# A reordered front, twenty zero products and a later overflow loop in a layer with a recurrence, cross-attention and 64 experts

## Chip, cores, metric

The kernel runs on one core of a Trainium2 chip. The metric is the device time of one execution in microseconds (us). A profile of one execution, taken by the hardware profiler, stands beside the times.

## What is computed

One layer for 256 tokens of width 1024, all in float32:

```python
u = rmsnorm(h, norm1_w)
rx, rg, qkv, z, a, b, ga, gb = split(u @ w_in)
rx = causal_dwconv(rx, w) + bias            # 4 taps
h_rnn = rglru(rx, ...)                      # linear recurrence along the tokens, 1280 channels
y_a = (gelu(rg) * h_rnn) @ w_branch_a
q, k, v = split(silu(causal_dwconv(qkv)))   # 8 heads of 128
o = gated_delta_rule(l2norm(q), l2norm(k), v, g(a), sigmoid(b))   # chunks of 64
y_b = (rmsnorm(o) * silu(z)) @ w_branch_b
h = h + (sigmoid(ga) * y_a + sigmoid(gb) * y_b) @ w_out
h = h + cross_attention(rmsnorm(h), rmsnorm(mem))   # 4 heads, 256 memory tokens
h = h + hier_moe(rmsnorm(h))  # best of 8 groups, then best 2 of its 8 experts; SwiGLU, 512 wide
return rmsnorm(h)
```

## The kernel before

The core has engines that run side by side, each with its own queue in a fixed order: TensorE (PE) multiplies, VectorE (DVE), ScalarE (ACT) and GpSimd (POOL) do the rest, and SyncE (SP) issues most loads. The program is written in a tile framework. A planner there fixes each engine's order ahead of time: it goes by the order in which the code names the operations, lets an operation inside `tc.high_priority()` go ahead, and puts a ready one in front of one that its own cost estimates hold to be late. Tiles come from pools with a few buffers, and a tile waits until the buffer's last user is done. A loop whose count is only known at run time (`tc.For_i`) is a block of its own, and nothing is planned across it.

*The front.* Its dense products come in units. A unit loads 1 MB of weights on SP (`load_w`, line 162), splits them into a high and a low half (`whl`: the high half on ACT, line 169; the low half for one part on DVE and for the other on POOL, line 170), and multiplies in 48 steps of 128 by 256 (`dense`, lines 178 to 180) into a bank of PSUM (`mm`, four of them). After that comes the unit's own work:

- 5 x units: the convolution (`conv`) on ACT and with six steps on DVE, into `xc`;
- 5 gelu units (`g_unit`): three steps on ACT and DVE in turn, into `gg`;
- `memory_norm` (the norm of the memory tokens, and keys `KT` scaled by it) and `smalls` (constants of the recurrence);
- `recurrence(h)`, twice, for five blocks of 128 channels each: 10 products into banks `gd` (line 385), tanh and exp on ACT (lines 386 to 393), eight long steps on DVE over 128 by 1280 (lines 394 to 404), a split into `ghh` and `ghl`;
- `decay` (the decay factors of the delta rule), and 4 value units (`value_unit`), which make the memory's values with one scaled copy on ACT;
- 12 k, q and v units (`qkv_unit`): convolution and SiLU on ACT and DVE at high priority, with `z_unit(0)` ahead of the second, `key_sums` behind the eighth (line 496) and `query_sums` behind the tenth (line 519);
- 8 short units for `wa`, which need both recurrences' results, then the delta rule with the remaining units, `wb`, `wo`, the attention, `wco`.

The order before is: x units with `memory_norm` behind the first, `smalls`, gelu units, both recurrences, `decay`, value units, and then the twelve units. Tiles of the front that live long come from a pool of ten buffers (`early`).

*The choice.* With the last `wco` unit the router's logits are done. Four PSUM banks `into` are opened with a product by zeros each (line 81). DVE then finds group and experts (lines 962 to 988, at high priority), TensorE counts the places of the tokens (lines 990 to 995), and `xe0`, the tokens of expert 0, is gathered (line 1045).

*The experts.* Each of 64 experts has three weight tiles of 2 MB (gate, up, down), 192 in all, which go through a ring of ten tiles: four in pool `ra`, six in pool `rb`, which lies where the front's weights were. `load_next` issues them on SP in order (lines 1101 to 1109); a load waits until its tile has been read by the expert ten tiles earlier. The expert `e` (`expert(e)`) multiplies its up to 32 tokens with gate and up (`gate_up`, line 1140, 64 products each), makes the hidden values, multiplies with down (line 1160) and keeps the rows in `Y`. After every fourth expert `combine` adds four experts' rows into `into` (line 1176), and `prepare` gathers the tokens of the next four into `xe`: two comparisons on DVE for every second call (line 1002), a scale (line 1123) and 32 products (line 1131).

*The overflow.* An expert with more than 32 tokens needs further blocks. Their number `nblk` is counted in the choice, and `overflow` runs a loop over it:

```python
n = nc.values_load(nblk[0:1, 0:1], ...)     # line 1235
with tc.For_i(0, n, 1):                     # line 1236
    ...                                     # picks the block's expert, loads its weights by SP, adds its rows
```

With these inputs the body isn't entered. It uses the memory of `xe` for its weights. Before, `overflow()` stands ahead of the experts.

Of the kernel before, what the change touches and what calls it, by code (L numbers as in the profile page):

```python
# [41 lines left out]
def hybrid_kernel(ctx: ExitStack, tc: tile.TileContext, A, out, dbg=None, until=99):  # L42
    nc = tc.nc
    V, SC, G, T = nc.vector, nc.scalar, nc.gpsimd, nc.tensor
# [291 lines left out]
    def smalls():  # L336

        V.tensor_scalar_mul(ch[:, 0], P("lam"), -1.0)
        softplus(ch[:, 1], ch[:, 0], ch[:, 2], ch[:, 3], ch[:, 4])
        V.tensor_scalar_mul(ch[:, 0], ch[:, 1], -4.0)  # L340
        V.tensor_scalar_mul(ch[:, 1], ch[:, 1], 2.0)
        V.tensor_scalar_mul(hb[:, 0], P("ba"), 0.5)
        V.tensor_scalar_mul(hb[:, 1], P("bx"), 0.5)
# [35 lines left out]
    def recurrence(h):  # L379
        tr, ti = five("tr"), five("ti")  # L380
        for b in range(HB):
            r = h * HB + b
            p = bank("gd")
            for s in range(2):
                T.matmul(p[:, s * 256:s * 256 + 256], wg[h][:, s, b], xc[h][:, b], start=True, stop=True)
                SC.activation((tr, ti)[s][:, b], p[:, s * 256:s * 256 + 256], AF.Tanh,
                              bias=hb[:, s, r:r + 1], scale=0.5)

        a = five("lra")
        for b in range(HB):  # L390
            r = h * HB + b
            SC.activation(a[:, b], tr[:, b], AF.Exp, bias=ch[:, 0, r:r + 1], scale=ch[:, 0, r:r + 1])
            SC.activation(tr[:, b], tr[:, b], AF.Tanh, bias=ch[:, 1, r:r + 1], scale=ch[:, 1, r:r + 1])
        V.scalar_tensor_tensor(tr, a, 1.0, tr, op0=OP.add, op1=OP.mult)
        V.tensor_scalar(a, tr, -1.0, 1.0, op0=OP.mult, op1=OP.add)
        V.scalar_tensor_tensor(tr, tr, -2.0, tr, op0=OP.add, op1=OP.mult)

        SC.activation(tr, tr, AF.Sqrt, scale=-1.0 / 16)
        V.scalar_tensor_tensor(ti, ti, 1.0, xc[h], op0=OP.add, op1=OP.mult)
        V.tensor_mul(ti, ti, tr)  # L400
        V.memset(a[:, :, 0:1], 0.0)
        flat = lambda t: t.rearrange("p b t -> p (b t)")
        V.tensor_tensor_scan(flat(tr), flat(a), flat(ti), 0.0, OP.mult, OP.add)
        V.tensor_mul(ti, tr, gg[h])
        dump(f"gh{h}", ti)
        hi, lo = five("ghh", FR), five("ghl", FR)
        split(hi, lo, ti)
        gh.append((hi, lo))
# [16 lines left out]

    for un_ in range(5):
        x_unit(un_)
        if un_ == 0:
            memory_norm()
    smalls()  # L430
    for un_ in range(5):
        g_unit(un_)
    for h in range(2):
        recurrence(h)
    decay()
    for un_ in range(4):
        value_unit(un_)
    if until <= 1:
        return

# [71 lines left out]
    def query_sums():  # L512
# [8 lines left out]
        V.tensor_scalar(NK[:, 1], pss[:, :16], 0.25, EPS, op0=OP.mult, op1=OP.add)  # L521
        V.tensor_scalar_mul(NK[:, 1], NK[:, 1], 2048.0 * EPS)

    for un_ in range(12):
        if un_ == 1:
            z_unit(0)
        qkv_unit(un_)
        if un_ == 7:
            key_sums()
        if un_ == 9:  # L530
            query_sums()
# [415 lines left out]

    into = [[opened(bank(), 512) for _ in range(2)] for _ in range(2)]


    LA = small("rla", [2, 72])
    LG, LE = LA[:, :, :8], LA[:, :, 8:].rearrange("p t (g j) -> p t g j", g=8)
# [235 lines left out]
    def prepare(k):  # L1188

        if k < NE // 4:  # L1190
            if k % 2 == 0:
                g, pw = picked if k == 0 else (onehot(k * 4, 8), None)
                pw = pw or weighted(k // 2, g)
                oh[k // 2] = g, pw.rearrange("p (t x) -> p t x", t=2)
            gather(xe, oh[k // 2][0][:, :, k % 2 * 128:k % 2 * 128 + 128], 128)

    def expert(e, last=None):
        g8, i = divmod(e, 8)
        x = xe[:, :, i % 4 * 32:i % 4 * 32 + 32] if e else xe0
        p = bank("gd")  # L1200
        for k in range(2):
            m = gate_up(p, k * 128, x, ring[3 * e + k], range(8))
        if e == 2:
            pin = tc.keep_in_program_order
            pin(m)
            for tt in range(2):
                for h in range(2):
                    pin(T.matmul(into[tt][h], ident, hm[:, tt].rearrange("p (c q) -> p q c", c=8)[:, h * 64:h * 64 + 64],  # L1208
                             start=False, stop=False, skip_group_check=True))
        ht = hidden(p)  # L1210
        if last:
            return last(ht, [last_columns(ring[3 * e + 2], q) for q in LAST])
        p = bank("gd")
        down(p, ht, ring[3 * e + 2], range(4))
        to_rows(Y, 32 * (i % 4), p)
        for _ in range(3):
            load_next()
        if i % 4 == 3 or e == NE - 2:
            n = 32 * (i % 4 + 1)
            combine(lambda tt: oh[g8][1][:, tt, 32 * (i + 1) - n:32 * (i + 1)], Y, n)  # L1220
        if e == 0:
            prepare(0)
        if i % 4 == 3:
            prepare(e // 4 + 1)

# [45 lines left out]
            to_rows(Y, 0, p)  # L1271
            combine(lambda tt: opw[:, tt], Y, SLOTS)

    overflow()
    for e in range(NE - 3):
        expert(e)

# [159 lines left out]
```

## Time and profile before

| | |
|---|---|
| time, median of 3 runs | 1500.93 us (1498.08 to 5531.12) |
| the profiled execution | 1499.66 us, span 1497.9 us |
| mean granted TensorE clock | 0.885 |
| busy: PE, DVE, ACT, POOL | 1109.8, 539.3, 349.4, 199.9 us |
| read from memory | 474.17 MB |

The span runs from the first to the last instruction of the profiled execution, and the time of that execution has a little around it. Busy shares are means over very different parts: in the front DVE and PE are busy, in the expert part the DMA engines.

### The profile page before, as it was taken

To read this page: it belongs to the slowest core of one execution; us is meant where nothing else is said; L and a number is where in the kernel's file an instruction comes from. 1 tells how busy PE (TensorE), PEld (TensorE's weight loads), DVE (VectorE), ACT (ScalarE), POOL (GpSimd) and SP (SyncE) were. 2 spreads that over 40 slices of the span, in tenths; PEclk is the share of its full clock that TensorE was granted. 3 is DMA by queue.
4 is the path that set the end of the run, shared out by engine and by line. 5 is a ranking of instruction groups with operands and counts; after the bars stand their busy time and mean duration, and the time that the engine had idled before them with its cause. 6 is when DMAs were issued, how large, how long until landed. Compare 5 with 4: busy or idle time off the path is not lost.

```text
span 1497.9 us, 33194 instructions
## 1 busy us (share of the span) xinstructions
PE 1109.8 (74%) x14941; PEld 929.0 (62%) x14941; DVE 539.3 (36%) x1217; ACT 349.4 (23%) x741; POOL 199.9 (13%) x107
## 2 busy tenths in 40 slices
PE   6998999979999957876565675756656756666575
PEld 6997999979889945654444553545544545445453
DVE  7966786675757332221111211111202111111122
ACT  5356664417435510100000000000000000000011
POOL 2443332621136200000000000000000000000000
PEclk9999998989999978998898887887979889789897
DMA  7343352521268367999999999999999999999994
GB/s 254 138 170 130 123 170 92 191 85 58 84 243 325 116 273 327 426 425 425 426 426 427 425 427 424 425 426 427 425 426 425 426 426 427 425 425 427 426 424 177
DMA packets 42002, 477.40 MB, mean 319 GB/s; under 512 B 4481, under 2 KB 7169, under 8 KB 9857
## 3 DMA queue, kind: packets, MB, share of 16 engines
q1 hardware_dynamic: 40560, 472.56, 76.9%
q8 instruction: 119, 1.95, 0.5%
q10 hardware_dynamic: 1296, 2.68, 0.5%
q14 instruction: 27, 0.21, 0.0%
HBM read 474.17 MB, written 1.05 MB: 317 GB/s over the span
## 4 chain that ended last, share of the span: by engine, by line
DMA 56%; PE 5%; DVE 0%; issue 0%; ACT 0%; DVEq 0%; SPq 0%; ACTq 0%
DMA rb<-wed 13%; DMA rb<-weu 11%; DMA rb<-weg 11%; DMA ra<-weu 8%; DMA ra<-weg 8%; DMA ra<-wed 5%; PE gd L1140 2%; PE gd L1160 1%; PE mm L1176 1%; PE gd L1131 1%; PE mm L1208 0%; ACT fsq L1329 0%; DVE goh L1002 0%; PE gd L1313 0%; PE mm L1322 0%
## 5 line engine op out<-in xcount | busy, mean ns | idle before, releaser
L1140 PE MATMUL gd<-rb,xy 128*32 128x128 f32 x4864 | 182.0, 314 | 112.7 <-DMA rb<-weu 56.8
L1140 PEld LDWEIGHTS gd<-rb,xy 128*32 128x32 f32 x4864 | 160.1, 127 | 140.1 <-DMA rb<-weu 65.0
L170 POOL TENSOR_TENSOR whl<-raw,whl 128x1024 fp32r<-128x1024 f32 (+1 forms) x66 | 161.5, 2448 | 328.5 <-ACT whl L169 324.9
L1149 DVE SCALAR_TENSOR_TENSOR hid<-hid,gd 128x128 f32<-128x128 f32 x64 | 18.4, 288 | 440.7 <-ACT hid L1148 440.7
L1140 PE MATMUL gd<-ra,xy 128*32 128x128 f32 x3168 | 120.3, 317 | 72.4 <-DMA ra<-weg 35.2
L180 PE MATMUL mm<-u1h,whl 128*128 128x256 f32 x544 | 159.0, 292 | 6.9 <-DVE whl L170 6.4
L1140 PEld LDWEIGHTS gd<-ra,xy 128*32 128x32 f32 x3168 | 106.3, 128 | 88.6 <-DMA ra<-weu 40.1
L179 PE MATMUL mm<-u1l,whl 128*128 128x256 f32 x544 | 159.9, 294 | 0.0
L178 PE MATMUL mm<-u1h,whl 128*128 128x256 f32 x544 | 159.4, 293 | 0.0
L169 ACT CAST whl<-raw 128x1024 fp32r<-128x1024 f32 (+1 forms) x132 | 131.1, 1007 | 118.5 <-PE mm L180 87.9
L1148 ACT ACTIVATE hid<-gd 128x128 f32<-128x128 f32 x64 | 17.7, 277 | 532.0 <-PE gd L1140 532.0
L1160 PE MATMUL gd<-rb,hid 128*32 128x256 f32 x1216 | 94.5, 463 | 62.9 <-DMA rb<-wed 44.2
L1165 DVE COPY xy<-gd 32x256 f32<-32x256 f32 x126 | 52.6, 418 | 236.0 <-PE gd L1160 209.4
L1165 ACT COPY xy<-gd 32x256 f32<-32x256 f32 x126 | 45.8, 364 | 314.8 <-DVE xy L1165 314.8
L180 PEld LDWEIGHTS mm<-u1h,whl 128*128 128x128 f32 x544 | 107.9, 198 | 8.3 <-DVE whl L170 7.0
L179 PEld LDWEIGHTS mm<-u1l,whl 128*128 128x128 f32 x544 | 108.1, 199 | 2.1 <-issue 1.7
L1160 PEld LDWEIGHTS gd<-rb,hid 128*32 128x32 f32 x1216 | 47.5, 128 | 99.1 <-issue 65.1
L178 PEld LDWEIGHTS mm<-u1h,whl 128*128 128x128 f32 x544 | 108.0, 198 | 1.1 <-issue 0.7
L1009 POOL TENSOR_TENSOR gpw<-goh,ew 128x512 f32<-128x512 f32 x8 | 8.4, 1046 | 747.2 <-PE sm L1171 680.3
L170 DVE TENSOR_TENSOR whl<-raw,whl 128x1024 fp32r<-128x1024 f32 (+1 forms) x66 | 82.2, 1246 | 55.3 <-ACT whl L169 54.9
L1160 PE MATMUL gd<-ra,hid 128*32 128x256 f32 x800 | 62.1, 462 | 38.7 <-DMA ra<-wed 19.6
L1131 PEld LDWEIGHTS gd<-goh,hm 128*128 128x128 f32 x512 | 61.5, 194 | 15.8 <-issue 15.8
(420 smaller groups left out, 1782.2 us busy)
## 6 DMA issues: line engine op xcount, KB each, us to landing
rb<-weu SPq DMA_DIRECT2D x38, 2048.0 KB, 39.8
rb<-wed SPq DMA_DIRECT2D x38, 2048.0 KB, 39.8
rb<-weg SPq DMA_DIRECT2D x38, 2048.0 KB, 39.8
ra<-weg SPq DMA_DIRECT2D x26, 2048.0 KB, 39.9
ra<-weu SPq DMA_DIRECT2D x25, 2048.0 KB, 39.8
ra<-wed SPq DMA_DIRECT2D x25, 2048.0 KB, 39.8
raw<-win SPq DMA_DIRECT2D x34, 1024.0 KB, 4.9
raw<-wkv SPq DMA_DIRECT2D x7, 1024.0 KB, 4.9
```

Of the source, the lines that this page charges most:

```text
L169: (hi[j].copy if hi[j] is SC else hi[j].tensor_copy)(w[:, 0], r)
L170: lo[j].tensor_sub(w[:, 1], r, w[:, 0].bitcast(FT))
L178: T.matmul(p, w(0, i, ms), u(0, i), start=(i == 0), stop=False)
L179: T.matmul(p, w(0, i, ms), u(1, i), start=False, stop=False)
L180: T.matmul(p, w(1, i, ms), u(0, i), start=False, stop=(i == k - 1))
L1131: T.matmul(o, hm[:, tt, c * 128:c * 128 + 128], g[:, tt], start=(tt == 0), stop=(tt == 1))
L1140: m = T.matmul(p[32 * j:32 * j + 32, o:o + 128], x[:, c], w(c)[:, j * 128:j * 128 + 128], start=(c == 0), stop=(c == 7), tile_position=(0, ...
L1148: SC.activation(tg, p[:, :128], AF.Tanh, scale=0.5)
L1149: V.scalar_tensor_tensor(th, tg, 1.0, p[:, :128], op0=OP.add, op1=OP.mult)
L1160: T.matmul(p[32 * q:32 * q + 32, :256], ht[:, 32 * j:32 * j + 32], w(j)[:, o:o + 256], start=(j == 0), stop=(j == 3), tile_position=(0, 32 ...
L1165: (SC.copy if q % 2 else V.tensor_copy)(Y[r:r + 32, q * 256:q * 256 + 256], p[32 * q:32 * q + 32, :256])
L1176: T.matmul(into[tt][h], ct[:n, tt * 128:tt * 128 + 128], Y[:n, h * 512:h * 512 + 512], start=False, stop=False, skip_group_check=True)
```

## The change

It moves calls and adds twenty products; no operation is taken out.

- x and gelu units alternate (x0, g0, x1, ...); `memory_norm` stands behind the second x unit instead of the first, `smalls` behind the fourth.
- Both recurrences, `decay` and the value units go into the loop over the twelve k, q and v units: `recurrence(0)` ahead of the first, `recurrence(1)` ahead of the third, a value unit behind each of the first four, `decay` behind the fifth. `z_unit(0)` goes from behind the first to behind the seventh.
- Behind the opening of the banks `into`, twenty products by zeros (128 by 128 by 512) are added into them.
- `overflow()` is called inside `expert(31)`, behind its `combine` and ahead of `prepare(8)`, and no longer ahead of the experts.

```diff
--- before.py
+++ after.py
@@ -425,16 +425,11 @@
 
     for un_ in range(5):
         x_unit(un_)
-        if un_ == 0:
+        if un_ == 1:
             memory_norm()
-    smalls()
-    for un_ in range(5):
+        if un_ == 3:
+            smalls()
         g_unit(un_)
-    for h in range(2):
-        recurrence(h)
-    decay()
-    for un_ in range(4):
-        value_unit(un_)
     if until <= 1:
         return
 
@@ -521,10 +516,17 @@
         V.tensor_scalar(NK[:, 1], pss[:, :16], 0.25, EPS, op0=OP.mult, op1=OP.add)
         V.tensor_scalar_mul(NK[:, 1], NK[:, 1], 2048.0 * EPS)
 
+
     for un_ in range(12):
-        if un_ == 1:
+        if un_ in (0, 2):
+            recurrence(un_ // 2)
+        qkv_unit(un_)
+        if un_ < 4:
+            value_unit(un_)
+        if un_ == 4:
+            decay()
+        if un_ == 6:
             z_unit(0)
-        qkv_unit(un_)
         if un_ == 7:
             key_sums()
         if un_ == 9:
@@ -947,6 +949,9 @@
 
     into = [[opened(bank(), 512) for _ in range(2)] for _ in range(2)]
 
+    for k in range(20):
+        T.matmul(into[k // 2 % 2][k % 2], zeros, zeros[:, :1].to_broadcast([128, 512]), start=False, stop=False, skip_group_check=True)
+
 
     LA = small("rla", [2, 72])
     LG, LE = LA[:, :, :8], LA[:, :, 8:].rearrange("p t (g j) -> p t g j", g=8)
@@ -1220,6 +1225,8 @@
             combine(lambda tt: oh[g8][1][:, tt, 32 * (i + 1) - n:32 * (i + 1)], Y, n)
         if e == 0:
             prepare(0)
+        if e == 31:
+            overflow()
         if i % 4 == 3:
             prepare(e // 4 + 1)
 
@@ -1271,7 +1278,6 @@
             to_rows(Y, 0, p)
             combine(lambda tt: opw[:, tt], Y, SLOTS)
 
-    overflow()
     for e in range(NE - 3):
         expert(e)
```

## Rows read from the trace of the kernel before

**Rows 1.** The chain that ended last, in order of time: start, length, what

```profile
633.40 37.90 DMA rb<-weu
...
1428.21 40.66 DMA rb<-wed
```

**Rows 2.** The page's part 2: bytes moved per second in 40 equal slices

```profile
GB/s 254 138 170 130 123 170 92 191 85 58 84 243 325 116 273 327 426 425 425 426 426 427 425 427 424 425 426 427 425 426 425 426 426 427 425 425 427 426 424 177
```

**Rows 3.** Timeline of SP's queue: start, length, the load issued

```profile
536.07 0.33 SPq L1106 DMA_DIRECT2D rb<-weu  x1
...
539.41 0.44 SPq L1106 DMA_DIRECT2D rb<-weg  x1
573.95 0.34 SPq L1101 DMA_DIRECT2D ra<-weu  x1
```

**Rows 4.** Windows: length, busy time by engine, granted clock, DMA share, GB/s

```profile
567.00:568.00 1.00, 0.00 (x0) 0.00 (x0) 0.00 (x0) 0.00 (x0) 0.00 (x0) 0.50 0.35 147
...
567.00:576.00 9.00, 5.56 (x132) 5.13 (x132) 0.30 (x1) 0.28 (x1) 0.00 (x0) 0.64 0.19 50
```

**Rows 5.** Timeline of the choice and expert 0, with idle time before and its releaser

```profile
536.00 0.82 PE L81 MATMUL mm<-zeros 128*128 128x512 f32 x3
...
544.17 0.69 PE L990 MATMUL sm<-ew,consts 128*128 128x64 f32 x2 [6.32 <-DVE ew L988]
...
550.07 0.42 DVE L1045 TENSOR_TENSOR xe<-gd,vecs 128x256 f32<-128x256 f32 x1 [1.44 <-PE gd L1044]
...
570.44 1.93 PE L1140 MATMUL gd<-ra,xe 128*32 128x128 f32 x32 [20.41 <-SPq L1236]
...
575.55 0.71 PE L1123 MATMUL sm<-goh,rs 128*128 128x128 f32 x4
...
575.70 0.43 DVE L1002 TENSOR_TENSOR goh<-rk,consts 128x256 f32<-128x256 f32 x1 [25.21 <-PE gd L1140]
...
579.21 3.90 PE L1131 MATMUL gd<-goh,hm 128*128 128x128 f32 x32
...
583.04 1.96 PE L1140 MATMUL gd<-ra,xy 128*32 128x128 f32 x64
```

**Rows 6.** Line 1236 on SP's queue: count, duration in ns, first and last start

```profile
L1236 SPq EVENT_SEMAPHORE  x1: 17/17/17, 559.6 to 559.6; - x1
...
L1236 SPq EVENT_SEMAPHORE  x1: 17/17/17, 564.5 to 564.5; - x1
...
L1236 SPq EVENT_SEMAPHORE  x2: 17/17/17, 569.4 to 569.5; - x2
```

**Rows 7.** Timeline of PE in the front: the products behind its longest waits

```profile
76.43 0.58 PE L180 MATMUL mm<-u1h,whl 128*128 128x256 f32 x1 [3.88 <-DVE whl L170]
...
148.91 1.65 PE L385 MATMUL gd<-xc,wax 128*128 128x256 f32 x3 [6.50 <-ACT tr L386]
...
186.81 0.39 PE L180 MATMUL mm<-u1h,whl 128*128 128x256 f32 x1 [1.94 <-DVE whl L170]
...
216.73 0.66 PE L496 MATMUL gd<-consts,kf 128*128 128x128 f32 x4 [2.51 <-ACT sqk L500]
...
245.13 1.24 PE L519 MATMUL sm<-ones,sqq 128*128 128x1 f32 x8 [2.14 <-ACT sqq L516]
```

**Rows 8.** Windows of the front: length, busy PE PEld DVE ACT POOL, clock, DMA, GB/s

```profile
51.30:113.30 62.00, 58.12 (x463) 57.87 (x463) 46.53 (x92) 28.82 (x37) 27.41 (x10) 0.94 0.44 152
113.30:155.60 42.30, 35.80 (x257) 33.63 (x256) 26.29 (x21) 29.27 (x52) 12.80 (x4) 0.92 0.34 120
155.60:239.50 83.90, 78.98 (x642) 78.35 (x641) 73.47 (x111) 52.59 (x104) 33.92 (x13) 0.98 0.42 143
239.50:279.20 39.70, 37.56 (x275) 37.24 (x273) 17.54 (x34) 18.42 (x31) 11.24 (x7) 0.83 0.44 150
```

**Rows 9.** Groups by line on DVE, 113.3:155.6 and 155.6:239.5: busy us, mean ns

```profile
L395 DVE TENSOR_SCALAR lra<-tr 128x1280 f32<-128x1280 f32 x1 | 3.0, 3033 | 0.0
...
L395 DVE TENSOR_SCALAR lra<-tr 128x1280 f32<-128x1280 f32 x1 | 0.8, 810 | 0.0
```

## Prediction

> **What bounds the kernel now.** I read the page first, for the end. The chain that ended last is one row of DMA pieces after another from 633 us on, some 40 us each, until expert work at 1469 us [rows 1]: the stream of expert weights. The bytes per second of the 40 slices show its limit: about 426 GB/s in every slice from the 17th to the last but one, and less before [rows 2]. So the program has two parts. In the front (0 to 536 us) TensorE works through dense products; then the stream runs, and the end comes when the last byte has come. A microsecond saved in the front counts if the stream starts that much earlier; a microsecond saved in the expert part counts only if the stream itself stood still in it.
>
> Next, the queue that issues the stream. The first six tiles of pool rb go out at 536 to 539 us, right behind the last dense unit, whose weight pools they replace; the next load is only issued at 573.95 us [rows 3]. Between the two the stream runs dry: data end about 0.35 us into 567:568, and of the 9 us from 567 to 576 only a share of 0.19 is used, so 9 × 0.81 = 7.3 us of the stream are lost [rows 4]. The timeline says why: expert 0's first product waited 20.4 us on SP's line 1236, the loop of `overflow`. Its body does not run (nothing of it lies between xe0 at 550 us and expert 0 at 570 us, [rows 5]), so this is the price of entering and leaving an empty loop. What it waits for is in SP's semaphore instructions on that line: at 559.6, 564.5 and 569.4 us, 4.9 us apart, and the last about 2 us after the data end [rows 6]. A tile of 2 MB at 426 GB/s takes 4.9 us. I conclude that the loop waits until every load in flight has landed, and that all engines stand at it.
>
> **The loop behind expert 31.** At the old place its price is the 7.3 us: 567.35 to 569.4 the last landing (2.05), to 570.44 the other engines (1.04), 64 products until the first tile is free at 573.95 (3.51), and 0.7 until bytes move again [rows 3 to 6]. Without the loop there, expert 0 can begin at 550.5 us on this run's clock and frees its first tile by 554, while rb tiles still arrive until 567. That gap goes: −7.3 us.
>
> At the new place the same thing happens in mid-stream. When expert 31 is done, ten tiles are loaded or in flight. The eleventh needs a tile that expert 32 reads, and expert 32 stands behind the loop. So the loop waits for all ten, some 45 us in which TensorE idles at no cost while data flow; then the stream stands until expert 32 has freed a tile. Before that comes what the old place did not have: `prepare(8)` stands behind the loop, and expert 32 needs its gather. By the rows of the gather after expert 0: two comparisons 2 × 0.43 = 0.86, the scale products 0.71, 32 gather products 3.90, then 64 gate products 1.96, or 6.57 on TensorE at 2.4 GHz [rows 5]. TensorE will have idled, so it starts at 1.2 GHz. In this trace the clock was at half until 573.5 us (mean 0.64 in 567:576, [rows 4]), 3.1 us after the first product; that costs 1.55 us here. Sum: 2.05 + 1.04 + 0.86 + 6.57 + 1.55 + 0.7 = 12.8 us. Lower end, full clock: 11.2; upper end, half clock throughout: 17.8. So moving the loop costs 12.8 − 7.3 = +5.5 us (+3.9 to +10.5). Behind the waiting SP stand only loads that have no free tile; ACT, DVE and POOL have nothing due.
>
> **The zeros in the choice.** 20 products of 512 columns, 0.27 us each by the opening of the same banks, 5.5 us in a hole of 6.3 us in which TensorE waits for the choice on DVE [rows 5]. They end about when the hole does. At half clock they would run 5 us over; but from 550 to 567 us the loads are covered, so even that reaches nothing. They keep the clock up into expert 0: its first 64 products took 3.51 us at half clock against 1.96 at full [rows 3, 5]. That is 1.55 us off TensorE, and 0 off the end, because the first six tiles are still landing. The Trainium skill (TensorE: Matmul & The Clock Gate, "Why this matters for your kernels") advises keeping TensorE busy so that its clock does not fall; by that alone 1.55 us would be gained, and by the row of the stream none. Cost and gain taken as 0.
>
> **The front.** Everything here is one chain on TensorE, so I list where TensorE stood still between 51 and 279 us: 3.88 us at 72.5 and 1.94 at 184.9 (for the low halves of weights that DVE makes), 6.50 at 142.4 (first products of the second recurrence), 2.51 at 214.2 (`key_sums`), 2.14 at 243 (`query_sums`) [rows 7]. After each the clock falls as well. One minus the mean clock, times the stretch, is what that costs: 0.06 × 62 = 3.7 us in 51.3:113.3, 0.08 × 42.3 = 3.4 in 113.3:155.6, 0.02 × 83.9 = 1.7 in 155.6:239.5, 0.17 × 39.7 = 6.7 in 239.5:279.2 [rows 8]. Waits and clock make 32.5 us, the most that the new order could save.
>
> *x and gelu alternating.* The stretch of the ten units has DVE busy 46.5 of 62 us [rows 8], crowded into the x units (30 convolution steps) with little in the gelu units. Ten units alternating spread that to 75%; the wait of 3.88 us and its 3.7 us of clock should go. `memory_norm` and `smalls` move inside that stretch with small DVE steps only; their DMAs are none. Taken: −7 (0 to −7.6).
>
> *Value units between k units, recurrence ahead.* In 113.3:155.6 DVE is busy 26.3 of 42.3 us, in 155.6:239.5 73.5 of 83.9 [rows 8]. Together 99.8 of 126.2, where TensorE needs 126.2 − 11.4 (busy against length of the two rows) − 5.1 (clock) = 109.7. Value units have almost no DVE work, k units much, so mixing them helps; but DVE would be 91% busy. The 6.50 us wait comes from the second recurrence being placed too early for the first one's buffers; with two k and two value units between them it should shrink, not surely vanish. It and its clock are worth 9.9 us; I take −6 (0 to −9.9). The waits at 184.9, 214.2 and 243 have causes that the change leaves in place: taken −1, from +11 (rival 2) to −15. `decay` (needed at `key_sums`) and z unit 0 keep their cover, TensorE's dense products; the four weight loads of the value units pass on SP in the new order, 1 MB each against a queue that is at 0.44 of its share or less here [rows 8].
>
> Front: −14 us, and the stream starts 14 us sooner.
>
> **The sum.** The profiled run took 1499.66 us (span 1497.9), 1.3 under the median of 1500.93, so I work from it: 1499.7 − 14 + 5.5 = 1491 us.
>
> **Rivals.**
> 1. *The loop at its new place leaves the stream running*, because ten tiles ahead are enough or it does not wait for all loads. For: TensorE has slack there. Against: rows 6 show it waiting landing by landing. Then 1499.7 − 14 − 7.3 = 1478 us.
> 2. *DVE becomes the bound of the front (slower).* The k units, value units and recurrence share a stretch in which DVE already has 91%. The same step (lra) took 3.03 us in one recurrence and 0.81 in the other [rows 9], so DVE work can stretch by POOL working beside it. The Trainium skill (SBUF — State Buffer, "Who interferes with whom") says that DVE and GpSimd lock one port pair for a whole instruction; the trace agrees, with these 3.03 and 0.81. It decides from the point where DVE needs more than TensorE's 109.7 us, 10% over its 99.8. Price: the stall at 184.9 with its clock (1.94 + 1.7 = 3.6 us) at each of the four pairs of units instead of once, +11 over now; with −7 from the x units, and the 6.50 staying, the front loses 4 us: 1499.7 + 4 + 5.5 = 1509 us. If the stalls merely return elsewhere, 1505.
> 3. *All front waits and clock losses go*: 1499.7 − 32.5 + 5.5 = 1473 us. Against: `key_sums` and `query_sums` stay where they are.
>
> **How the numbers follow.** Forecast 0.5 (1483 to 1500), rival 1 0.18, rival 2 0.22, rival 3 0.10. The range 1473 to 1508 takes in rival 3, rival 1 and the milder end of rival 2, and the bounds of the loop's gap; it leaves out the harsher half of rival 2 (0.1) and rivals 1 and 3 together (1460, 0.06). 2% is about 30 us, what a measurement here can tell from no change: faster 0.06, same 0.92, slower 0.02.
>
> **What would show it.** Right: expert 0 begins within 2 us of xe0; no dry stretch before the 11th load; instead, near 976 us (86 loads of 4.92 us after the tenth tile's data at 553), some 45 us with all engines idle and then a dip of 11 to 18 us in the stream; rb loads issued near 522 us; no wait of TensorE for weights among the x units. Wrong: no dip in the stream (rival 1), rb loads at or after 536 us with many DVE waits of TensorE among the k units (rival 2), or near 504 us (rival 3).

## The result and the profile after

| | before | after |
|---|---|---|
| time, median of 20 runs each | 1497.6 us (1495.2 to 5531.1) | 1509.2 us (1500.5 to 1513.9) |
| ratio | | 1.0063, 95% interval 1.0051 to 1.0075 |
| the profiled execution | 1499.66 us, span 1497.9 | 1512.37 us, span 1510.6 |
| mean granted clock | 0.885 | 0.879 |

The change costs 0.6% by this ratio and 11.6 us (0.8%) between the medians, less than the 2% that count as a difference here; 1491 us had been forecast. (The ratios here and in the table of experiments are not quotients of the medians; where a kernel has two groups of times, the two differ.) One thing shows only in the single times. Seven of the 20 runs of after lie between 1500.5 and 1503.9 us, thirteen between 1508.7 and 1513.9, none between. Of 133 runs of before taken in this study (one of 5531 us left out) three lie 7 us or more above the quickest of their batch, the rest within that. The profile of after shows a run of the upper group.

The page's clock and bytes in 40 slices of after, against [rows 2]:

```profile
PEclk9999987968999989998887888885998898889798
...
GB/s 250 166 168 115 137 150 96 175 84 57 41 214 320 186 211 424 426 424 426 426 425 426 426 426 426 424 424 343 328 425 423 428 425 425 426 426 425 426 426 239
```

The stream starts with the 16th slice, as before, and it now has a dent in the 28th and 29th (343 and 328): the loop. SP's queue in after, against [rows 3]:

```profile
546.30 0.33 SPq L1111 DMA_DIRECT2D rb<-weu  x1
...
549.68 0.45 SPq L1111 DMA_DIRECT2D rb<-weg  x1
564.90 0.33 SPq L1106 DMA_DIRECT2D ra<-weu  x1
```

The front ended 10.2 us later than before (546.30 against 536.07), where 14 us sooner had been forecast. The eleventh load follows 15 us later and not 35. Windows of after (length, busy time by engine, granted clock, DMA share, GB/s), against [rows 4]; the last two are where the loop stands now:

```profile
549.00:579.00 30.00, 24.34 (x386) 19.92 (x384) 14.21 (x71) 2.34 (x8) 1.50 (x2) 0.83 1.00 424
1046.00:1055.00 9.00, 0.00 (x0) 0.00 (x0) 0.00 (x0) 0.00 (x0) 0.00 (x0) 0.50 0.46 197
1055.00:1066.00 11.00, 9.58 (x164) 9.47 (x164) 2.44 (x8) 0.28 (x1) 0.00 (x0) 0.75 0.10 20
```

No gap is left at the start of the stream (share 1.00). The new one loses 9 × 0.54 + 11 × 0.90 = 14.8 us, forecast at 12.8. The timeline of TensorE there, the loop's semaphores on SP's queue (line 1243 in this kernel, against [rows 6]), and the first load behind it:

```profile
1056.42 1.22 PE L1128 MATMUL sm<-goh,rs 128*128 128x128 f32 x4 [41.98 <-SPq L1243]
1057.43 5.21 PE L1136 MATMUL gd<-goh,hm 128*128 128x128 f32 x32
1062.57 3.70 PE L1145 MATMUL gd<-rb,xy 128*32 128x128 f32 x128
...
L1243 SPq EVENT_SEMAPHORE  x1: 17/17/17, 1045.6 to 1045.6; - x1
...
L1243 SPq EVENT_SEMAPHORE  x1: 17/17/17, 1050.5 to 1050.5; - x1
...
1064.59 0.34 SPq L1111 DMA_DIRECT2D rb<-weu  x1
```

TensorE stands 42 us at the loop while tile after tile lands, 4.9 us apart. Then come the scale, the gather and the gate products, and only then a load. TensorE's long waits in the front of after, against [rows 7]:

```profile
68.53 0.61 PE L349 MATMUL sm<-ones,nx 128*128 128x1 f32 x4 [2.29 <-DVE nx L214]
...
112.41 0.92 PE L385 MATMUL gd<-xc,wax 128*128 128x256 f32 x3 [1.57 <-ACT tr L386]
...
147.45 0.79 PE L385 MATMUL gd<-xc,wax 128*128 128x256 f32 x1 [6.06 <-ACT tr L386]
...
189.62 0.60 PE L303 MATMUL sm<-xg,consts 128*64 128x12 f32 x4 [5.27 <-ACT egl L297]
...
235.31 1.01 PE L514 MATMUL sm<-ones,sqq 128*128 128x1 f32 x4 [2.93 <-ACT sqq L511]
```

The waits for weights are gone (3.88, 1.94), as is that of `key_sums` (2.51). New are one for the norm of the memory (2.29), one at the first recurrence (1.57) and one for `decay` (5.27); the second recurrence still waits 6.06 where it waited 6.50. That is 18.1 us in five waits for 17.0 in five. The windows of the same stretches, against [rows 8], and one more:

```profile
51.30:113.30 62.00, 57.87 (x469) 56.96 (x468) 49.42 (x85) 32.83 (x45) 30.45 (x11) 1.00 0.45 154
113.30:155.60 42.30, 36.24 (x261) 34.49 (x260) 31.64 (x32) 30.84 (x53) 12.62 (x5) 0.92 0.36 125
155.60:239.50 83.90, 75.43 (x598) 74.59 (x597) 69.81 (x106) 50.93 (x103) 29.01 (x12) 0.91 0.40 132
239.50:279.20 39.70, 39.70 (x303) 39.57 (x304) 15.05 (x26) 16.07 (x25) 11.47 (x8) 0.85 0.44 148
279.20:360.00 80.80, 71.07 (x567) 69.14 (x563) 52.99 (x121) 20.88 (x33) 31.61 (x19) 0.77 0.26 91
```

The clock is better in the first stretch (1.00 for 0.94) and worse in the third (0.91 for 0.98). The wa units end at 278.91 us, before at 279.24: up to there the new order won 0.3 us in this pair. (Other profiles of the two orders of the front have 276.2 to 277.8 for the new one and 277.9 to 279.4 for the old one, so about 1 us.) The 10 us are lost behind that, in the delta rule, in which the change altered nothing; there the mean clock is 0.77 in the last row and was 0.92 before. TensorE waits 7.6 us for DVE there in both kernels (line 630 before, 632 after). That wait in before, and the 33 us behind it in before, in after, and in after once more, from the second profile (e8):

```profile
322.02 1.30 PE L630 MATMUL gd<-stt,ab 128*128 128x64 f32 x5 [7.58 <-DVE stt L610]
...
322.00:355.00 33.00, 32.90 (x244) 32.17 (x245) 18.55 (x33) 12.20 (x34) 2.37 (x1) 0.86 0.16 62
```

```profile
321.40:354.40 33.00, 33.00 (x157) 33.00 (x157) 11.79 (x17) 2.85 (x4) 0.73 (x1) 0.51 0.08 30
```

```profile
318.50:351.50 33.00, 32.91 (x237) 32.22 (x238) 17.70 (x33) 11.35 (x31) 2.37 (x1) 0.83 0.17 62
```

After the length, the first column is TensorE's: busy all 33 us in each, but with 157 products at half clock in place of 237 or 244.

### The profile page after: what moved, and what is told of

Its sections match the earlier page's. It is cut to its first block, busy times and chain, and to the rows that moved or that the text cites. A ratio compares the mean times of both kernels' runs of the same rounds, so it can differ in the third digit from the quotient of the medians.

```text
span 1510.6 us, 33221 instructions
## 1 busy us (share of the span) xinstructions
PE 1116.1 (74%) x14961; PEld 937.9 (62%) x14961; DVE 538.9 (36%) x1217; ACT 349.0 (23%) x741; POOL 198.7 (13%) x107
## 3 DMA queue, kind: packets, MB, share of 16 engines
q8 instruction: 119, 1.95, 0.5%
## 5 line engine op out<-in xcount | busy, mean ns | idle before, releaser
L180 PE MATMUL mm<-u1h,whl 128*128 128x256 f32 x544 | 162.1, 298 | 1.1 <-DVE whl L170 0.8
L178 PE MATMUL mm<-u1h,whl 128*128 128x256 f32 x544 | 162.5, 299 | 0.0
L1145 PE MATMUL gd<-ra,xy 128*32 128x128 f32 x3168 | 114.2, 305 | 63.6 <-DMA ra<-weu 31.2
L1145 PEld LDWEIGHTS gd<-ra,xy 128*32 128x32 f32 x3168 | 99.9, 123 | 79.8 <-DMA ra<-weu 36.0
L180 PEld LDWEIGHTS mm<-u1h,whl 128*128 128x128 f32 x544 | 110.1, 202 | 2.5 <-DVE whl L170 1.2
L178 PEld LDWEIGHTS mm<-u1h,whl 128*128 128x128 f32 x544 | 109.9, 202 | 1.5 <-issue 0.7
L1139 DVE SCALAR_TENSOR_TENSOR xy<-gd,vecs,rr 128x128 f32<-128x128 f32 x128 | 39.0, 347 | 108.7 <-PE gd L1136 108.2
```

The lines of the kernel that those rows point to most:

```text
L178: T.matmul(p, w(0, i, ms), u(0, i), start=(i == 0), stop=False)
L180: T.matmul(p, w(1, i, ms), u(0, i), start=False, stop=(i == k - 1))
L1139: V.scalar_tensor_tensor(xe[:, c], p[:, m * 256:m * 256 + n], P("w3", c), rr, op0=OP.mult, op1=OP.mult)
L1145: m = T.matmul(p[32 * j:32 * j + 32, o:o + 128], x[:, c], w(c)[:, j * 128:j * 128 + 128], start=(c == 0), stop=(c == 7), tile_position=(0, ...
```

## The experiments

Two theories were put against each other. *A*: the reordered front neither wins nor loses by itself; the loss is the loop (a few us) and, in the upper group of runs, the clock that stays at half behind the delta rule's wait (called the long case below). *B*: the work order is the loss, with DVE as the bound of the front (rival 2 of the prediction). "Late" in the table counts runs 7 us or more above the quickest of the same row.

| | kernel | median us | ratio to before, 95% | late |
|---|---|---|---|---|
| e1 | before + loop at expert 31 | 1502.6 | 1.0021 to 1.0045 | 0 of 6 |
| e2 | before + front | 1506.0 | 1.0010 to 1.0055 | 8 of 12 |
| e3 | before + x and gelu alternating | 1497.7 | 0.9990 to 1.0023 | 2 of 12 |
| e4 | before + zeros | 1497.9 | 0.9993 to 1.0010 | 0 of 11 |
| e5 | after + fill | 1519.2 | 1.0121 to 1.0160 | |
| e6 | before + fill | 1518.1 | 1.0110 to 1.0145 | |
| e7 | before, loop in expert 0 | 1495.5 | 0.9973 to 0.9992 | 0 of 11 |
| e8 | after again | 1503.2 | 1.0028 to 1.0075 | 2 of 6 |
| e9 | before, delay 2 | 1498.4 | 0.9975 to 1.0019 | 1 of 12 |
| e10 | before, delay 7 | 1501.7 | 1.0017 to 1.0064 | 5 of 12 |
| e11 | after, delay 7 | 1503.8 | 1.0025 to 1.0066 | 3 of 12 |
| e12 | after, recurrence later | 1494.9 | 0.9959 to 0.9999 | 1 of 12 |
| e13 | e12, loop in expert 0 | 1490.2 | 0.9930 to 0.9956 | 0 of 5 |
| e14 | e13, norm as before | 1486.1 | 0.9896 to 0.9925 | 0 of 5 |
| e15 | before, one recurrence later | 1502.4 | 1.0008 to 1.0034 | 11 of 12 |
| e16 | e1, loop ahead of its loads | 1497.5 | 0.9983 to 1.0000 | 0 of 11 |
| e17 | after, unchanged | 1503.9 | 1.0021 to 1.0058 | 1 of 6 |
| e18 | e14, unchanged | 1484.4 | 0.9888 to 0.9918 | 1 of 4 |

**e1 to e4: the parts alone.** Each is the kernel before with one part of the diff: the call of `overflow()`, the whole front, only the loop over x and gelu units (with `memory_norm` and `smalls` in it), the zeros.

> The kernel before with one part of the change: the overflow loop behind expert 31. Theory A (the loop's move costs little, the rest of the loss is elsewhere): the gap of 7.5 us behind the tenth load goes, a gap of 15 us comes near 1055 us, and some 5 us are given back at the end of the stream, so +2.4 us against before, about 1500. Rival B (the loop is the main loss): the gap counts in full and nothing is given back at the end, +8 us, about 1505.5.

> The kernel before with the whole reorder of the front, the loop and the choice as before. Theory A: up to 279 us the reorder gains nothing (waits and clock losses only move), and the loss arises later, in the delta rule, where the granted clock comes back either early or late behind the same wait for DVE; so the runs fall into two groups, near 0 and near +10 us against before (1497 and 1507). Rival B (DVE bounds the reordered front, so the front is slower by its own work): every run +8 to +11 us, one group, and the end of the wa units comes 8 to 11 us later than 279 us.

> The kernel before with x and gelu units alternating and the norm of the memory and the constants of the recurrence at their new places; all else as before. The prediction's own term: -7 us (1490). Theory A: the wait of 3.9 us and its clock loss go, so the gelu units end 4 to 5 us sooner, and what comes behind keeps its waits; the end is then -4 us, or up to +8 where the clock in the delta rule comes back late. Rival B (the units gain, and the gain is lost at the recurrence in any order): the end of the wa units stays at 279 us, 0 us.

> The kernel before with the twenty products by zeros alone. Both theories: the clock stays up through the choice, expert 0's first 64 products take 2 us in place of 3.5, and the first tile is free that much sooner behind the loop, where in this order the stream stands: 0 to -1.5 us against before. A rival: the zeros delay the counting of the places behind them, +1 to +5 us.

e1 measures the loop at +4.9 us (+3.1 to +6.7). The end of its stream, and its gap:

```profile
1471.00:1497.00 26.00, 17.27 (x216) 10.04 (x208) 8.39 (x28) 6.00 (x16) 0.00 (x0) 0.76 0.48 172
1034.00:1055.00 21.00, 10.78 (x166) 10.23 (x166) 2.45 (x9) 0.55 (x2) 0.00 (x0) 0.63 0.26 98
```

The gap is 21 × 0.74 = 15.5 us. At the end the DMA engines idle 26 × 0.52 = 13.5 us from the last full slice on; in before 35 × 0.53 = 18.6 (a window from 1460 to 1495 us with a share of 0.47). So 15.5 − 7.3 − 5.1 = +3.1, at the low end of what the times say. e2 falls into two groups, four runs from 1495.2 to 1499.2 and eight from 1504.8 to 1510.8; its wa units end at 277.8 us, so the front is not slower by its own work, and B's one group 8 to 11 us up is not there. e3 alone moves nothing: the gelu units end 2.4 us sooner (111.1 for 113.5), and the second recurrence begins at 147.3, 1.7 sooner; the wait of 3.88 us is gone, and `memory_norm` makes TensorE wait 3.25 us in its place. e4 is 0 within 0.1%.

**e8: the changed kernel once more.** No edit.

> The changed kernel again, for a second profile. Theory A: its runs fall again near 1501 and near 1510 us, and the profile shows the half clock behind the delta rule's wait either for 37.6 us, or for about 14 us with a time near 1502. Rival B: a quick run differs from a slow one in the front ahead of 279 us, or in the loop's gap.

Four runs at 1501.5 to 1503.2, two at 1510.9 and 1511.6; the profiled one took 1501.48 us. Its first rb load, and its products behind the wait beside those of the first profile of after, each with the granted clock of two stretches:

```profile
534.30 0.33 SPq L1111 DMA_DIRECT2D rb<-weu  x1
...
318.52 7.06 PE L632 MATMUL gd<-stt,ab 128*128 128x64 f32 x32 [7.59 <-DVE stt L612]
...
327.62 2.79 PE L632 MATMUL gd<-stt,yb 128*128 128x64 f32 x16
...
330.65 1.89 PE L632 MATMUL gd<-stt,yb 128*128 128x64 f32 x16
...
315.84:329.47 13.63, 10.95 (x52) 10.98 (x52) 7.10 (x11) 0.00 (x0) 0.00 (x0) 0.50 0.24 78
329.50:351.50 22.00, 21.93 (x187) 21.22 (x187) 13.26 (x26) 11.35 (x31) 2.37 (x1) 1.00 0.14 48
```

```profile
321.39 7.06 PE L632 MATMUL gd<-stt,ab 128*128 128x64 f32 x32 [7.59 <-DVE stt L612]
...
330.49 3.51 PE L632 MATMUL gd<-stt,yb 128*128 128x64 f32 x16
...
334.54 3.51 PE L632 MATMUL gd<-stt,yb 128*128 128x64 f32 x16
...
316.42:353.95 37.53, 32.56 (x153) 32.59 (x153) 16.56 (x28) 2.42 (x3) 0.28 (x1) 0.50 0.09 29
353.97:360.00 6.03, 5.96 (x50) 5.52 (x49) 3.56 (x9) 4.52 (x15) 2.05 (x1) 1.00 0.47 168
```

One program, the same wait to 0.01 us, and the same sixteen products in 1.89 or 3.51 us. The clock records have half clock from 315.83 on, within the wait, for 13.65 us here, and from 316.41 for 37.55 there. From the end of the wait to the first rb load e8 takes 215.8 us, the first profile 224.9: 9.1 us, and the two groups' medians are 8.4 apart (1510.6 and 1502.3). The front up to that wait was 2.9 us quicker in e8 besides, so two runs of one program differ there too. Of the eighteen profiles with this wait of 7.6 us (all but e5 and e6), those of the six late runs (after, e2, e10, e11, e15, e18) have the long stretch, and the twelve others the short one: the upper group is that stretch of half clock.

**e5 and e6: filling the wait.** 30 products by zeros behind the dense units that stand ahead of the wait, in after and in before:

```diff
     meanwhile(4)
+    pf = bank()
+    for k in range(30):
+        T.matmul(pf, zeros, zeros[:, :1].to_broadcast([128, 512]), start=(k == 0), stop=(k == 29), skip_group_check=True)
```

> The changed kernel with 30 products by zeros of 512 columns laid into the 7.6 us in which TensorE waits for DVE in the delta rule (314 to 321 us); nothing else is altered. Theory A (the loss of the change is the clock that stays at half for 37.6 us behind that wait): with TensorE busy in the wait the clock stays at full, so the runs form one group, some 19 us under the profiled run of the changed kernel, near 1492 us, and 6 to 7 us under its quick runs. Rival B (the loss is DVE's work in the front and the loop's gap): the same time as the changed kernel, 1509.

> The kernel before with the same 30 products by zeros in the same wait of the delta rule. Theory A: the 13.7 us at half clock behind that wait go, which costs half as much again as they last in TensorE's work, -6 to -7 us, about 1491. Rival B (that stretch is bound by DVE, not by TensorE's clock): 0 us.

Both expectations failed: both kernels end about 20 us above before, e5 10 us above after's median. TensorE in e6, with its clock in the 33 us behind:

```profile
312.28 6.72 PE L624 MATMUL mm<-zeros 128*128 128x512 f32 x30
322.77 0.44 PE L634 MATMUL gd<-stt,ab 128*128 128x64 f32 x1 [3.77 <-DVE stt L610]
...
322.80:355.80 33.00, 33.00 (x155) 33.00 (x156) 11.44 (x18) 0.83 (x2) 0.00 (x0) 0.50 0.08 30
```

The planner took the zeros for more work and put dense products of the delta rule's stretch into another order, 3.8 us of wait stayed, and the clock stayed at half all the same. They say nothing for B, and they don't show that a busy TensorE would keep its clock there. e17 and e18 were to try that with every order unchanged, by slower products ahead of the wait:

> The changed kernel with every engine's order unchanged, and 32 products of the last two dense units ahead of the delta rule's wait taken in plain float32 (the same sum, 0.31 us slower each, 10 us in all): TensorE works through the wait of 7.6 us and is about 2.4 us later than DVE. Theory A (the half clock behind that wait is the loss): it stays at full clock there, so 6.8 us (quick runs) to 18.8 us (late runs) at half clock go for 2.4 us of work, one group near 1497, 12 us under the changed kernel's median. Rival B (DVE and the order of work are the loss): 2.4 us more than now, 1504 and 1512 in two groups.

> The kernel of e14 with the same 32 slower products, every engine's order unchanged against e14. Theory A: 6.8 us of half clock go for 2.4 us of work, -4 us against e14, 1482. Rival B: +2.4 us, 1488.5.

But the edit's numbers reached another parameter of `dense`, and both ran the very instructions of after and of e14. They are repeats, and whether TensorE can be kept at full clock over that wait stays untried. As repeats they count: with e17, 16 of 32 runs of after are in the upper group, and e18's profile is a late run of the kernel of e14 (clock 0.52 in the 33 us behind the wait, where e14's profile has 0.86).

**e9 to e11: the same orders, shifted.** Some products of the sixth wa unit are taken in plain float32, the same sum done slower. Every engine's order stays as it was.

```diff
-            T.matmul(p, w(0, i, ms), u(0, i), start=(i == 0), stop=False)
+            f = (lambda t: t.bitcast(FT)) if i < slow else (lambda t: t)
+            T.matmul(p, f(w(0, i, ms)), f(u(0, i)), start=(i == 0), stop=False)
...
-        dense(p[:, m % 2 * 256:m % 2 * 256 + 256], w, 0, lambda s, i: gh[i // HB][s][:, i % HB], k=RB)
+        dense(p[:, m % 2 * 256:m % 2 * 256 + 256], w, 0, lambda s, i: gh[i // HB][s][:, i % HB], k=RB,
+              slow=2 if m == 5 else 0)     # e9; 7 in e10 and e11
```

> The kernel before, with every engine's order unchanged, and two products of the sixth wa unit taken in plain float32, which is the same sum done slower: some 0.7 us more work ahead of the delta rule. Theory A (where the wait of the delta rule falls against the clock decides whether half clock lasts 14 or 38 us behind it): a shift so small brings before into the late case, so most runs +9 to +10 us (1507), with 37.6 us at half clock behind the wait. Rival B (the loss of the change comes from its order of work, and before has nothing of it): +0.7 us, 1498.5, all runs.

> The same with seven such products, some 2.3 us more work ahead of the delta rule, the order of every engine again unchanged. Theory A: the larger shift leaves the late case again, so +2.3 us (1500), all runs, and less than with two products. Rival B: +2.3 us, and more than with two.

> The changed kernel, with every engine's order unchanged, and the same seven products in plain float32: some 2.3 us more work ahead of the delta rule. Theory A: the shift takes the changed kernel out of the late case, so the runs form one group near 1503 us, the quick runs' 1501 and 2.3 on top, and the median falls by 5 to 6 us from 1509 although work was added. Rival B: 1511, 2.3 us above the changed kernel.

I had the shift that turns before late wrong: the small one left it alone (1 of 12), the larger one made 5 of 12 late, against 2 of 35 runs of before taken beside it and 3 of 133 in all. e11 has 3 of 12 late and a median 5.4 us under after's first 20 runs, but the repeats without any edit (e8, e17) have 3 of 12 late as well and medians of 1503.2 and 1503.9. So it isn't shown that the shift did anything in after; what is shown is that after's share of late runs differs from batch to batch. e10's profile fell on a late run; the 33 us behind its wait:

```profile
322.40:355.40 33.00, 33.00 (x161) 33.00 (x161) 11.79 (x17) 2.84 (x4) 0.73 (x1) 0.52 0.08 31
```

That is the row of after, from the program before with about 2.2 us of extra work (seven products, each about 0.3 us slower) and its order unchanged.

**e12 and e15: where the second recurrence stands.** e12 is after, e15 before, with these calls moved:

```diff
# e12
-        if un_ in (0, 2):
-            recurrence(un_ // 2)
+        if un_ in (0, 4):
+            recurrence(un_ // 4)
+        if un_ == 0:
+            decay()
...
-        if un_ == 4:
-            decay()
# e15
-    for h in range(2):
-        recurrence(h)
+    recurrence(0)
...
+        if un_ == 2:
+            recurrence(1)
```

> The changed kernel with the second recurrence ahead of the fifth of the twelve units in place of the third, and the decay factors right behind the first recurrence in place of behind the fifth unit. Theory A (TensorE's waits of 6.06 us at 141 and of 5.27 us at 184 come from where these two stand, not from too much DVE work): both waits go, with up to 8 us of half clock, and the wa units end 11 to 15 us sooner than at 279 us; the end is 11 to 15 us sooner too, give or take the 9 us of the delta rule's clock. Rival (DVE bounds this stretch): the waits return at other units and the wa units end near 279 us again.

> The kernel before with one call moved: the second recurrence ahead of the third of the twelve units, everything else of the front in its old order. Theory A (the wait of 6.5 us at 142 comes from that place alone; between the two recurrences there are then four value units, two k units and a z unit, as against two and two in the change): the wait and its 3.4 us of half clock go, -9 us (1489). Rival (only the mixing of value and k units frees DVE): the wait returns at other units, 0 us.

e12's windows over the same two stretches as above, and its second recurrence, without a wait:

```profile
113.30:155.60 42.30, 39.34 (x327) 38.31 (x325) 33.58 (x38) 30.34 (x49) 14.28 (x6) 1.00 0.36 125
155.60:239.50 83.90, 77.47 (x599) 75.98 (x599) 63.60 (x100) 54.80 (x112) 33.33 (x14) 0.95 0.42 145
...
167.21 1.02 PE L385 MATMUL gd<-xc,wax 128*128 128x256 f32 x4
```

The waits of 6.06 and 5.27 are gone (one of 3.46 at `key_sums` and one of 1.94 for weights come in), the clock is 1.00 and 0.95 where it was 0.92 and 0.91, and the wa units end at 269.5 us, 9.4 sooner than after and 9.8 sooner than before. The same DVE work fits into less time, so DVE was no bound of this stretch: B falls. The median is 7.4 us under after's lower group. e15 has the wa units at 272.6, 6.7 sooner than before, and is still slower than before: eleven runs at 1500.6 to 1504.3, one at 1491.8. Its wait of 6.50 us is gone with that one move. In its profile the 33 us behind the delta rule's wait are at 0.52: a front that is 7 us shorter was more than paid back by the long case.

**e7 and e16: the loop at other places.**

```diff
         to_rows(Y, 32 * (i % 4), p)
+        if e == 0:          # e7; 31 in e16
+            overflow()
         for _ in range(3):
             load_next()
```

> The kernel before with the overflow loop called inside expert 0, behind its products and ahead of its own three loads, and with the routing factors in a small tile of their own. The loop's body isn't entered with these inputs; if it were, it would overwrite rows that are still needed here. Theory A (the loop's price is the landing of all loads, plus the work up to the first free tile): three tiles are free when the loop ends, so the loads go out at once and the gap shrinks from 7.5 us to 3.8 us (2.05 landing, 1.04 engines, 0.7 first bytes), -3.7 us. Rival B (the end of the stream gives or takes back what the gap loses): 0 us.

> The kernel of e1 with the loop some lines earlier in expert 31: ahead of the expert's own three loads in place of behind its combine. Its body isn't entered; if it were, it would overwrite rows still needed here. Theory A (the gap is landing, engines and first bytes, and behind them the gather and the gate products until a tile is free): three tiles are free when the loop ends, so of the 15.8 us the gather's and the gate's 7 to 10 us go; about 1495, -8 us against e1 and 3 under before. Rival (the gap is mostly the uneven end of the loads in flight, which waiting brings wherever it stands): -2 us against e1, 1500.5.

The call ahead of the experts goes in both; in e7, e13 and e14 the counts `cf`, which the loop's body reads, also get a tile of their own. e7 is 2.7 us under before, of the 3.7 expected; its gap is 4.9 us (9 us with a share of 0.46) in place of 7.3. e16, with TensorE's first product behind the loop, SP's first load and the windows of the gap:

```profile
1035.37 0.69 PE L1171 MATMUL sm<-consts,gpw 128*128 128x128 f32 x2 [37.29 <-SPq L1238]
...
1036.12 0.34 SPq L1109 DMA_DIRECT2D rb<-wed  x1
...
1025.00:1038.00 13.00, 2.63 (x8) 2.01 (x9) 0.76 (x2) 0.37 (x1) 0.00 (x0) 0.50 0.38 146
1038.00:1049.00 11.00, 11.00 (x167) 8.41 (x165) 2.43 (x8) 0.28 (x1) 0.00 (x0) 0.91 0.95 380
```

The load goes out 0.75 us behind the loop, where after's went 8.2 us behind it. The gap is 13 × 0.62 + 11 × 0.05 = 8.6 us, 6.9 less than in e1, and the median 5.2 less. So about 7 of the 15 us were the gather and the gate products ahead of the first load, and about 8 the landing of the loads in flight and the start.

**e13 and e14: the mended places together.** e13 is e12 with the loop as in e7; e14 has `memory_norm` behind the first x unit again (`if un_ == 0:`).

> The kernel of e12 (the changed kernel with the second recurrence ahead of the fifth unit and the decay factors behind the first recurrence), with the loop inside expert 0 as in e7 in place of behind expert 31. The loop's body isn't entered; if it were, it would overwrite rows still needed here. Theory A: e12's 1494.9, less the loop's 4.9 of e1 and the 2.3 gained in e7: 1487.5, 10 us under before, apart from runs 9 us later where the clock of the delta rule comes back late. Rival B (the parts don't add up, since an earlier front only makes the stream's end wait elsewhere): 1492 to 1495.

> The same, with the norm of the memory back behind the first x unit. Theory A: its wait of 2.3 to 3.3 us at 65 us and 1.7 us of half clock go, -4 us against e13 (1483.5). Rival: the wait for the low halves at 72 us comes back instead, 0 us.

1490.2 and 1486.1 us, each within 3 us of its expected sum, and −4.1 from one to the other. Where these 4 us come from isn't shown: in e14's profile the wait of 2.29 for `memory_norm` is gone, but 3.85 us for weights stand at the old place again, as the rival had it, and the wa units end at 270.5 us, in e13 at 270.0. e14 beats before by 0.8 to 1.0% and after by more. With the loop at these places (e7, e13, e14, e16) its body would spoil rows that are still needed if an expert had over 32 tokens, so they are measurements, not kernels to keep; e12 has no such flaw.

## Why the prediction was wrong

**The clock of the delta rule, not in the sum at all.** The prediction took TensorE's stretches up to 279 us one by one and let everything behind them shift as a block. In the upper group of runs the same program then spends 34 to 38 in place of 13.7 us at half clock from a wait on that the change didn't touch, and the end comes 8 to 9 us later. That is most of the 11.6 us between the medians, and it is why even the range failed: the lower group's median, 1502.3, and the medians of the two later batches of after (1503.2 and 1503.9, with 3 of 12 late) lie inside it. Shown: the two cases of one program (e8, e18 against e14), and that edits ahead of the wait move the odds (e2, e10, e15). Not shown: what decides the case in a run; the shift I guessed from the two first profiles was wrong (e9). One pattern stands in the clock records of the eighteen profiles, seen afterwards and tested by no run: in the twelve short cases the clock falls 2.69 to 4.86 us before the wait ends, and in the six long ones outside of that, 2.34 and 2.51 us or 4.90, 4.98, 5.69 and 5.70 us before it.

**The front, −14.** This step failed. *Alternating, −7*: the wait of 3.88 did go, and the gelu units ended 4.6 us sooner (108.8 for 113.5; 3.4 in e8 and 2.4 in e3, where the clock of the stretch stayed at 0.94). `memory_norm`, taken to bring small steps only, made TensorE wait 2.29 us in its place. And the next thing that TensorE needed was not TensorE's: the second recurrence's products wait for the first recurrence's chain of tanh, exp and scan on ACT and DVE, and they began at 147.5 in after, 147.3 in e3 and 148.9 before, so 1.5 us were left. The prediction gave the whole wait as won without asking for what is late next. *Mixing, −6*: the wait of 6.50 was to shrink behind two k and two value units; it is 6.06. Two more of each (e12) removed it. *`decay` keeps its cover*: wrong, moved behind the fifth unit it made TensorE wait 5.27 us and cost the clock behind. Sum: −0.3 at the wa units, about −1 over all profiles, where −14 stood in the sum. With the two calls moved (e12) the wa units end 9.8 us sooner than before, so most of the 14 us was there to be won, by another order.

**Rival 2** named the time (1505 to 1509) and not the cause. Its milder end, that the stalls merely return elsewhere, is what happened ahead of 279 us; its mechanism, DVE as the bound, is refuted by e12, and its price, a stall at each pair of units, is nowhere in the rows. The step of L395 that it leaned on ([rows 9]) averages 818 ns in after, but its neighbours are stretched there, L394 and L396, which take 1.49 us in the first recurrence of before:

```profile
L394 DVE SCALAR_TENSOR_TENSOR tr<-lra,tr 128x1280 f32<-128x1280 f32 x2 | 6.2, 3098 | 0.4 <-ACT tr L393 0.3
L396 DVE SCALAR_TENSOR_TENSOR tr<-tr 128x1280 f32<-128x1280 f32 x2 | 4.8, 2390 | 0.0
...
L395 DVE TENSOR_SCALAR lra<-tr 128x1280 f32<-128x1280 f32 x2 | 1.6, 818 | 0.0
```

So the stretching stayed, but it did not grow: the sixteen long steps of both recurrences together take 40.4 us before, 35.3 in after and 37.7 in e12. The Trainium skill (SBUF — State Buffer, "Who interferes with whom") explains such a stretched step by the port pair that DVE and GpSimd share; as a price for the front it would have added what did not come.

**The loop, +5.5**: measured +4.9. The mechanism stood: no gap ahead of the eleventh load, expert 0 at 561.2 right behind xe0 at 560.7, TensorE idle 42 us (forecast 45), then a dip. The work from the loop's end to the next load took 8.2 us (forecast 9.0). The size of the gap, 12.8, was 14.8 to 15.5: the data ran at half rate for the last 9 us before the loop ended (197 GB/s from 1046 to 1055), 4.9 us lost where 2.05 stood in the sum. The 5 us given back at the end of the stream were not in it either; their cause was not traced. The two misses nearly cancel, so that the sum came so near is in part luck.

**The zeros, 0**: right in the sum (e4), but they do not keep the clock up into expert 0. In after it is at half when expert 0 begins:

```profile
560.72 0.42 DVE L1050 TENSOR_TENSOR xe<-gd,vecs 128x256 f32<-128x256 f32 x1 [1.00 <-PE gd L1049]
...
561.20 4.07 PE L1145 MATMUL gd<-ra,xe 128*32 128x128 f32 x72 [0.52 <-DVE xe L1050]
...
561.20:564.80 3.60, 3.60 (x68) 3.34 (x72) 0.00 (x0) 0.00 (x0) 0.18 (x1) 0.50 1.01 428
```

The first 64 products take 3.64 us there, 1.95 in e8, and 1.95 in e1, which has no zeros. The end doesn't depend on it, because the loads are covered. The Trainium skill's advice to keep TensorE busy (TensorE: Matmul & The Clock Gate, "Why this matters for your kernels") was worth nothing here, where the stream is the bound, as [rows 3] had it: e4 is 0 within 0.1%.

**The base.** The sum started from 1499.7 us, 2.1 above the median of 1497.6 that 20 runs of before gave. With that, the terms close: 1497.6, less 1 for the front, plus 4.9 for the loop is 1501.5, where the lower group has 1502.3; the long case adds the rest.

## What to carry to other kernels

When a wait goes, look for what the next consumer waits for: a chain on other engines that starts no earlier keeps its end, and the gain with it. A run-time loop costs the landing of every load in flight and the work up to the next issued load, so put it where free tiles wait for loads. Where one program has two groups of times, take profiles of both before explaining a difference of their size; a reorder can cost or gain it without touching the place where it arises.

## What the runs showed of the hardware that was not expected

Around one wait of 7.6 us, with TensorE busy all the 33 us behind it, the granted clock went to 1.2 GHz and stayed there for 13.7 us, or for 34 to 38. All profiles of these kernels fall in one case or the other: a mean of 0.83 to 0.87 with 237 to 245 products in those 33 us, or 0.50 to 0.52 with 155 to 161. The end of a drain before a loop isn't always sharp: in mid-stream (after) the last 9 us ran at 197 of 426 GB/s, while ahead of expert 0 (before) 415 GB/s held from 537 to 567 us. Stretched DVE steps are common in the recurrences: four to six of sixteen in the profiles of before, after and e12, most of them steps of 1.49 us that took 2.1 to 3.5.
